# Which engine waits for the last store: the final wait of a row-sum kernel moved from SyncE to ScalarE

## Chip, cores, metric

One core of one Trainium2 chip. The metric is the device time of one execution in microseconds (us); all runs below are in the fast state, with a granted clock of 1.000. "Span" is the time from the first to the last instruction of the program in a profiled execution. The reported time is longer than the span, and that difference turns out to be what this case is about.

## The reference

```python
x = np.random.randn(32, 512, 1024).astype(np.float32)
relu_x = np.maximum(x, 0)
return np.sum(relu_x, axis=-1).astype(np.float32)
```

67.11 MB come in, 16,384 sums (0.07 MB) go out.

## The kernel before

SyncE issues all loads and all three stores. ScalarE clamps blocks in place and VectorE sums them; in the tail both take single rows with a fused sum. Loads raise one semaphore each, ScalarE raises `act`, VectorE raises `dve`, and the stores raise `stored`. At the end the kernel puts its semaphores back to zero. It writes that ending itself, without a barrier of its own:

```python
    # (cut: the body; n_stores is 3)
    nc.cur_bb = nc.bb_map[tc.start_bb_name + "_end"]
    nc.cur_bb.bb.instructions.clear()
    nums = sorted(s.num for s in (*sems.loads, sems.act, sems.dve))
    cleared = range(nums[0], nums[-1] + 1)
    assert len(cleared) == len(nums)
    nc.sync.sem_clear(cleared)
    nc.sync.wait_ge(sems.stored, 16 * n_stores).then_inc(sems.stored, -16 * n_stores)
    open_without_barrier(tc, EARLY)
    # (cut)

    # the end of the body (cut):
    act_row(buf[:, c + 3, :], m + 3, last_loaded)      # ScalarE's last work
    store(0, ROWS, *freed[0])
    store(ROWS, NT - ROWS - 2, *sums_done)
    # (cut: VectorE's last sums)
    store(NT - 2, 2, n_act, n_dve)                     # waits for act and dve
    return n_store
```

The clearing is safe where it stands: the last store of SyncE waits for all of `act` and `dve`, so nobody waits on a cleared semaphore any more.

## Time and profile before

| | before |
|---|---|
| reported time, three runs | 161.29 us (161.23 to 161.38) |
| reported time of the profiled run | 161.02 us |
| its span | 159.7 us (159.674 in the trace) |
| last sum of VectorE ends | 158.215 us |
| last store has landed | 159.641 us |
| SyncE's wait ends, the last instruction | 159.674 us |

The busy rows, the end of the chain and the two lines L45 and L46 are shown in the prediction below. How to read them: an instruction's duration does not contain the wait before it (L46 shows 17 ns, and SyncE's wait of 1.0 us stands as a gap in front of it). The profile's views show no instruction after the wait on L46.

### The profile page before, as it was taken

What the parts mean: (1) busy time and instruction counts of PE and PEld (TensorE: products, weight loads), DVE (VectorE), ACT (ScalarE), POOL (GpSimd) and SP (SyncE); (2) the same over time, 40 slices, a digit from 0 to 9 for tenths busy, and PEclk for the clock granted to TensorE, in tenths of its full rate; (3) what the DMA queues carried; (4) which work ended last, traced back from release to release, by engine and by line L of the source; (5) the groups of instructions that cost most, each with busy time, mean ns of one, the idle gap of its engine ahead of it and who ended that gap; (6) DMA issues with size and microseconds to landing.
All of it is one profiled execution on the core that took longest, in us unless ns stands there. A gap on an engine that the chain in (4) does not pass through costs nothing.

```text
span 159.7 us, 118 instructions
## 1 busy us (share of the span) xinstructions
DVE 117.5 (74%) x41; ACT 104.2 (65%) x50; POOL 0.2 (0%) x4
## 2 busy tenths in 40 slices
DVE  0000000009999499994999999999999999999986
ACT  3000059990799708996099941999339992499985
POOL 0000000000000000000000000000000000000000
DMA  8996996996996998979969969969969969898994
GB/s 279 509 525 263 525 525 263 525 525 263 525 493 296 525 410 378 525 345 443 525 263 525 525 263 525 525 263 525 525 263 525 525 263 525 345 443 386 409 408 126
DMA packets 2305, 67.18 MB, mean 421 GB/s; under 512 B 641, under 2 KB 897, under 8 KB 1025
## 3 DMA queue, kind: packets, MB, share of 16 engines
q1 hardware_dynamic: 2304, 67.18, 98.0%
q14 instruction: 1, 0.00, 0.0%
HBM read 67.11 MB, written 0.07 MB: 421 GB/s over the span
## 4 chain that ended last, share of the span: by engine, by line
DMA 43%; DVE 34%; ACT 17%; another core or an unknown queue 3%; SPq 1%; issue 0%; DVEq 0%
DMA io<-in_x_dram 43%; DVE res L123 32%; ACT io L115 17%; DVE io L140 1%; SPq L97 1%; DVE piece L219 0%; DVE piece L140 0%; DVEq L218 0%
## 5 line engine op out<-in xcount | busy, mean ns | idle before, releaser
L123 DVE TENSOR_REDUCE res<-io 128x8 f32<-128x8192 f32 (+2 forms) x9 | 101.1, 11287 | 39.9 <-ACT io L115 39.9
L115 ACT ACTIVATE io<-io 128x8192 f32<-128x8192 f32 (+2 forms) x9 | 81.7, 9110 | 47.6 <-DMA io<-in_x_dram 47.6
L130 ACT ACTIVATE io<-io 128x1024 f32<-128x1024 f32 x20 | 20.9, 1045 | 5.9 <-DMA io<-in_x_dram 5.7
L140 DVE TENSOR_SCALAR_CACHE_REDUCE io<-io 128x1024 f32<-128x1024 f32 (+1 forms) x14 | 15.5, 1165 | 0.7 <-DMA io<-in_x_dram 0.6
L130 ACT ACTIVATION_READ_ACCUMULATOR io<-io 128x1 f32 x20 | 3.8, 188 | 0.0
L115 ACT ACT_TABLE_LOAD x1 | 1.3, 1283 | 0.1
L140 DVE DVE_READ_ACCUMULATOR io<-io 128x1 f32 x14 | 1.1, 82 | 0.0
L219 DVE TENSOR_SCALAR_CACHE_REDUCE piece<-piece 128x406 f32<-128x406 f32 x1 | 0.6, 576 | 0.1
L140 DVE TENSOR_SCALAR_CACHE_REDUCE piece<-piece 128x260 f32<-128x260 f32 x1 | 0.4, 424 | 0.0
L264 POOL MEMSET const-bfloat16-1.0<- 128x1 bf16 x1 | 0.1, 101 | 0.0
L264 POOL MEMSET const-uint8-127<- 128x1 uint8 x1 | 0.1, 101 | 0.0
L264 POOL MEMSET const-float32-0.0<- 128x1 f32 x1 | 0.1, 98 | 0.2 <-issue 0.2
L264 POOL MEMSET const-float32-1.0<- 128x1 f32 x1 | 0.1, 98 | 0.0
L140 DVE DVE_READ_ACCUMULATOR piece<-piece 128x1 f32 x1 | 0.1, 83 | 0.0
L219 DVE DVE_READ_ACCUMULATOR piece<-piece 128x1 f32 x1 | 0.1, 83 | 0.0
## 6 DMA issues: line engine op xcount, KB each, us to landing
io<-in_x_dram SPq DMA_DIRECT2D x1, 4096.0 KB, 21.6
io<-in_x_dram SPq DMA_DIRECT2D x1, 2048.0 KB, 26.1
io<-in_x_dram SPq DMA_DIRECT2D x1, 1204.0 KB, 28.6
io<-in_x_dram SPq DMA_DIRECT2D x1, 512.0 KB, 29.4
piece<-in_x_dram SPq DMA_DIRECT2D x1, 202.0 KB, 29.3
piece<-in_x_dram SPq DMA_DIRECT2D x1, 130.0 KB, 29.3
io<-in_x_dram SPq DMA_DIRECT2D x7, 26.9
out_dram<-res SPq DMA_DIRECT2D x1, 55.0 KB, 1.6
```

The source lines that it names most:

```text
L97: dma = nc.sync.dma_start(out=dst, in_=src)
L115: i = nc.scalar.activation(out=ap, in_=ap, func=RELU)
L123: nc.vector.tensor_reduce(out=res[:, m : m + n], in_=ap, axis=mybir.AxisListType.X, op=ADD).wait_op(sems.act, n_act, "sem-ge").then_inc(se ...
L130: i = nc.scalar.activation(out=ap, in_=ap, func=RELU, accum_out=res[:, m : m + 1])
L140: i = nc.vector.tensor_scalar(out=ap, in0=ap, scalar1=0.0, scalar2=None, op0=MAX, op1=ADD, accum_out=accum_out,)
L219: nc.vector.tensor_scalar(out=last[:, :], in0=last[:, :], scalar1=0.0, scalar2=None, op0=MAX, op1=ADD, accum_out=res[:, NT - 2 : NT - 1],) ...
L264: nc = _bacc.Bacc("TRN2", target_bir_lowering=False, num_devices=1)
```

## The change

The wait for the stores, with its taking down of `stored`, goes from SyncE to ScalarE. SyncE's program then ends with the clearing. The evident intent is to let SyncE close its program while the store is still in flight.

```diff
     nc.sync.sem_clear(cleared)
-    nc.sync.wait_ge(sems.stored, 16 * n_stores).then_inc(sems.stored, -16 * n_stores)
+    nc.scalar.wait_ge(sems.stored, 16 * n_stores).then_inc(sems.stored, -16 * n_stores)
     open_without_barrier(tc, EARLY)
```

## The prediction

Its sum came to 161.29 - 0.07 = 161.22 us, its range to 160.9 to 161.5. The 0.07 us of the lean was worked out from no number.

> **What bounds the kernel now.** I first read the page, to see which resource is full over the whole span:
>
> ```profile
> span 159.7 us, 118 instructions
> DVE 117.5 (74%) x41; ACT 104.2 (65%) x50; POOL 0.2 (0%) x4
> ...
> DMA  8996996996996998979969969969969969898994
> ...
> q1 hardware_dynamic: 2304, 67.18, 98.0%
> ```
>
> Neither compute engine is full (74% and 65%), while the packets of the one queue take 98.0% of the time of 16 DMA engines. All the input, 67.11 MB of it, has to come in once, and the DMA row is high from the first slice to the last but one. The kernel is therefore bound by its loads, followed by a short tail: what has to be done with the last piece after it lands. A change can gain in the load stream or in that tail.
>
> The change touches only the last instructions, so I read the chain of work that ended last, at its end, and beside it the timeline of the last microseconds:
>
> ```profile
> 126.81 28.57 DMA io<-in_x_dram
> 155.39 0.02 issue
> 155.41 1.68 DVE io L140 x4
> 157.09 0.43 DVE piece L140 x2
> 157.51 0.03 issue
> 157.54 0.02 DVEq L218
> 157.56 0.07 issue
> 157.63 0.58 DVE piece L219 x2
> ```
>
> ```profile
> 157.67 0.18 ACT L130 ACTIVATION_READ_ACCUMULATOR io<-io 128x1 f32 x1
> 158.13 0.08 DVE L219 DVE_READ_ACCUMULATOR piece<-piece 128x1 f32 x1
> 158.24 0.33 SPq L108 DMA_DIRECT2D out_dram<-res  x1
> ```
>
> The chain's printed part stops with VectorE's last sum at 158.21, yet the span is 159.7: about 1.5 us follow. ScalarE is done at 157.67 + 0.18 = 157.85 and idle after that; VectorE's last read ends at 158.13 + 0.08 = 158.21; SyncE then issues the last store, from 158.24 to 158.57. What happens after this only the views of single lines show: the issues of DMAs with their time to landing, the two lines that the change touches (L45 is the clearing, L46 the wait), and SyncE's own waits:
>
> ```profile
> out_dram<-res SPq DMA_DIRECT2D x1, 1.0 KB, 1.4
> ```
>
> ```profile
> L45 SPq EVENT_SEMAPHORE_RANGE_CLEAR  x1: 58/58/58, 158.6 to 158.6; - x1
> ```
>
> ```profile
> L46 SPq EVENT_SEMAPHORE  x1: 17/17/17, 159.7 to 159.7; - x1
> ```
>
> ```profile
> SPq L46 <- SPq L46: 1.0, 1, 1.0
> ```
>
> The last store lands at about 158.24 + 1.4 = 159.64. SyncE clears the 15 load, act and dve semaphores at 158.6 in 58 ns, then waits 1.0 us for the landing, and its 17 ns instruction at 159.7 ends the program. The clearing lies wholly inside the flight of the store: it was already free.
>
> [...]L46 shows 17 ns, and the wait of 1.0 us only as a gap in front of it. [...]What there is, is a difference: the reported median is 161.29 us and the span 159.7, some 1.6 us more (1.3 us for the profiled execution itself, which took 161.02).
>
> **The change part by part.**
> Removed from SyncE: one wait with its update, L46. Its own duration is 17 ns, and the 1.0 us before it is waiting. It was the last instruction of SyncE, so nothing on SyncE comes earlier by its removal except the end of SyncE's program: from 159.67 to the end of the clearing, 158.6 + 0.06 = about 158.68, so 1.0 us earlier.
> Added to ScalarE: the same wait with the same update, behind its last read of the accumulator at 157.85. It gets to the wait about 159.64 - 157.85 = 1.8 us before the semaphore is full. Nothing of ScalarE's work lies behind it, and no work is delayed.
> Moved: the end of the program, from SyncE to ScalarE. How fast does ScalarE's sequencer wake? The trace before has no lone semaphore instruction on ScalarE, but it has three on SyncE (L107, 17 ns each) and one on VectorE (L218, 21 ns, 157.54, after the read that released it ended at about 157.50, so some 0.04 us of delay). For SyncE the same delay is 158.24 - 158.21 = 0.03 us at the last store; ScalarE's activations show a 0.02 us "issue" piece between a landing and a start in the chain. So the wake-up may differ by 0.00 to 0.02 us, and the instruction by 0.00 to 0.01 us.
> Not moved: all loads, all stores, every semaphore number, all work of VectorE and ScalarE before 157.85. The loads stay on SyncE's queue in the same order, and the store that is waited for is issued at the same moment by the same engine. The first 158.6 us should be the same in both traces.
> The sum inside the span: 159.67 + (-0.01 to +0.03) = 159.66 to 159.70, no change that 0.1% could show.
> Outside the span: the part after the last instruction can depend on which engine arrives last. [...]I lean to a small gain of some 0.07 us, for two reasons, neither of them in the trace: SyncE, which issued all the DMAs[...], is now free 1.0 us before the end, and someone who has already tuned the kernel moved the wait on purpose. 161.29 - 0.07 = 161.22.
>
> **The rivals.**
> (a) The clearing was on the path, and the change takes 1.0 us or more off the end. For it: by the trace SyncE's program does end 1.0 us earlier. Against it: the clear ends at 158.68 and the store lands at 159.64, and the program's end still needs that landing. If ending a program on SyncE cost much more than on ScalarE, all of the 1.3 us outside the span would be the most there is to win: 161.29 - 1.3 = 160.0, or -0.8%. Even this stays within 2%.
> (b) ScalarE is slow to end: [...]its own closing work is longer than SyncE's, and now it begins last. For it: before, ScalarE had 1.8 us between its last work and the end, in which any such thing was hidden. Against it: its sequencer merely waits, and by 159.64 its pipeline has been empty for 1.8 us.[...]
> (c) The load stream falls into another rhythm, because the program differs by one instruction per engine. For it: the load stream is 98% of the span, so a small share of it would outweigh all of the above. Against it: the difference comes after the last load, and the three runs before lie within 161.23 to 161.38. I give it the noise of runs, 0.1 to 0.2 us.
> (d) The early end of SyncE disturbs something that is still in flight, because its semaphores are cleared[...] before the store lands. The clearing was ahead of the landing before, too[...].
>
> **Range and chances.** The three runs before spread over 0.15 us. To this I add [...]a little more on the fast side for a part of rival (a) than on the slow side for (b): 160.9 to 161.5. To be faster by over 2% would need 3.2 us, twice all that lies behind VectorE's last sum within the span; to be slower by over 2% would need a new wait of 3.2 us, and nothing in the program makes one. I give each 0.6%, for surprises in the measurement.
>
> **What would show it right or wrong.** In the changed trace: the last loads land and VectorE's last read ends at 158.2 within 0.1 us; SyncE's last instruction is the clearing near 158.6, 58 ns long; a semaphore instruction of about 20 ns stands on ScalarE at 159.65 to 159.7 and is the last of all; the last store takes 1.4 us to land; the span is 159.7 within 0.1 us. If the span is equal and the reported time is not, the difference lies behind the program, in the order of arrival. The prediction is wrong if the time moves by more than 0.4 us: then ending on one engine costs more than on another, or the wait on ScalarE is satisfied later than the landing explains.

## The result

| | before | after |
|---|---|---|
| reported time, median of six fast runs each | 161.22 us (161.16 to 161.38) | 161.39 us (161.31 to 161.62) |
| span of the profiled run | 159.674 us | 159.866 us |
| its reported time minus its span | 1.35 us | 1.51 us |

Ratio 1.0011, interval 0.9998 to 1.0024: the same within 2%, and if anything slower. A ratio here is worked out from the single fast runs, so it is not quite the ratio of the medians.

First question: is it in the span? The page of the changed kernel has the same work and the same full DMA row:

```profile
span 159.9 us, 118 instructions
DVE 117.5 (74%) x41; ACT 104.2 (65%) x50; POOL 0.2 (0%) x4
...
DMA  8996996996997999989979969969969969898993
```

The chain of work that ended last (start, length, what), first of the kernel before and then of the changed one, says where most of the 0.19 us of span comes from:

```profile
0.43 40.65 DMA io<-in_x_dram
```

```profile
0.43 40.82 DMA io<-in_x_dram
41.25 0.02 issue
41.27 13.86 ACT io L115
...
126.99 28.58 DMA io<-in_x_dram
155.57 0.02 issue
155.59 1.68 DVE io L140 x4
157.27 0.43 DVE piece L140 x2
157.69 0.03 issue
157.72 0.02 DVEq L218
157.74 0.07 issue
157.81 0.58 DVE piece L219 x2
```

The wait for the first load is 0.17 us longer (40.82 against 40.65), and every later piece keeps its length: 28.58 against 28.57, 1.68 against 1.68, 0.43 against 0.43. The changed instruction stands 159 us after this. So most of the difference of these two spans comes in with the first load, and only a repetition can say whether that is chance.

Second, the end. These are the views of lines L45 and L46 and the last store's row among the DMA issues, of the changed kernel:

```profile
L45 SPq EVENT_SEMAPHORE_RANGE_CLEAR  x1: 58/58/58, 158.8 to 158.8; - x1
```

```profile
L46 ACTq EVENT_SEMAPHORE  x1: 17/17/17, 159.8 to 159.8; - x1
```

```profile
out_dram<-res SPq DMA_DIRECT2D x1, 1.0 KB, 1.4
```

As predicted: the clearing is SyncE's last instruction, the wait stands on ScalarE, takes 17 ns, and is the last of all; the store lands after the same 1.4 us. From the landing to the end of the wait the trace has 0.033 us before (159.641 to 159.674) and 0.038 us after (159.828 to 159.866). ScalarE wakes as fast as SyncE, to 5 ns.

Third, what lies behind the span. The packed trace lists only instructions that have a line of the program, and none stands there. But it keeps updates of semaphores, also of those that the program does not own (its own are 99 to 114). No view of `prof` prints them; they were read from the trace file itself. Semaphore 2 is such a one. These are its updates, in us from the end of the program's last instruction:

```
before, end 159.674:  three updates earlier, at 157.962, 158.001, 158.360 of the span, then
                      0.132 0.175 0.213 0.247 0.296 | 1.077 1.112 1.150 1.194 1.217 1.316 1.354 1.388 1.435
after,  end 159.866:  none earlier at the end of the program, then
                      0.139 0.178 0.222 0.245 0.343 0.383 0.417 0.463 | 1.248 1.283 1.321 1.364 1.388 1.487 1.525 1.559 1.606
```

Between the two groups most of the semaphores 7 to 255 get an update each (in the kernel before, from 0.26 to 0.85 us after the end). The trace does not say what semaphore 2 is for. The author took nine updates of it for one barrier, at which the engines wait for each other, and the passing from engine to engine for a walk; these are names for what the updates and e3 to e8 show, and nothing else about it is known here. The group on the right is a whole walk: nine updates in 0.358 us, on both kernels with the same steps to 1 ns. The one on the left is the same walk as far as it still had to go when the program ended. One more update of this walk stands at 0.449 us of the span, in both: an engine that has nothing to do had arrived at once. (TensorE has no instruction in either trace, and GpSimd's last ends at 0.43 us; that the update is TensorE's is shown by e5 below.)

So the author read the walk as one that visits the engines in a fixed order and waits at each for its end, which e3 to e5 then tested. Before, three engines had passed during the tail: updates at 157.962 (0.11 us after ScalarE's last work, 157.854), at 158.001 and at 158.360 (0.145 us after VectorE's, 158.215). That reads as TensorE (idle, at 0.449 us), ScalarE, GpSimd, VectorE, and then SyncE. When SyncE ended last, five updates were left, and the walk was done 0.296 us after the end. When ScalarE ended last, it was held at its second station, eight updates were left, and it was done after 0.463 us: 0.167 us more. After it, all takes the same 1.14 us in both (1.435 - 0.296 and 1.606 - 0.463). The two medians differ by as much (161.39 - 161.22 = 0.17), but that they agree so closely is partly luck: the same comparison gives 0.24 us in e2 and 0.05 us in e7 below. The part behind the span is steadier. The record gives every timed run's span, to 0.1 us; the mean of reported time minus span is 1.50 us over the six runs of the changed kernel, and 1.35 and 1.36 us over the two sets of nine runs of the kernel before on the chips of the experiments.

### The profile page after: what moved, and what is told of

Its sections match the earlier page's. It is cut to its first block, busy times and chain, and to the rows that moved or that the text cites. A ratio compares the mean times of both kernels' runs of the same rounds, so it can differ in the third digit from the quotient of the medians.

```text
span 159.9 us, 118 instructions
## 1 busy us (share of the span) xinstructions
DVE 117.5 (74%) x41; ACT 104.2 (65%) x50; POOL 0.2 (0%) x4
## 4 chain that ended last, share of the span: by engine, by line
DMA 43%; DVE 34%; ACT 17%; another core or an unknown queue 3%; SPq 1%; issue 0%; DVEq 0%
DMA io<-in_x_dram 43%; DVE res L123 32%; ACT io L115 17%; DVE io L140 1%; SPq L97 1%; DVE piece L219 0%; DVE piece L140 0%; DVEq L218 0%
```

## Experiments

**Theory A, the walk**: the order of the engines in the closing barrier makes the difference. Rivals: **B, the load stream**: the difference is chance in the first loads. **C, SyncE's early end**: it is not ScalarE's place that costs, but that SyncE closes while a store is in flight. And the prediction's own rival (b): ScalarE is slow to close. Each kernel below has the reference's output, and was right. In each, five runs were timed beside nine of the kernel before on the same chip. The first four kernels share one chip and its nine runs of before (median 161.14 us), the other four another (161.25 us). In the expectations "before" is the kernel before, and the times "to the release" and "to the end of the last barrier" count from the end of the program's last instruction to the last update of the left and of the right group above.

**e1: the kernel before against itself.** No edit.

> The kernel before, unchanged, against itself: the noise of the comparison. Theory A (the walk): the program is followed by a barrier that goes from engine to engine, seen in the trace as nine rises of one semaphore; with SyncE last, four of the nine lie before the last instruction's end or wait on nothing, so the time from the end of the program to the end of the last barrier is 1.43 us (1.435 in the trace of before) and reported time minus span 1.35 us. Theory B (the load stream): the 0.17 us between the two kernels is chance in the loads, so this run should itself scatter by 0.1 to 0.2 us in its span. Both: ratio 1.000 within 0.001.

Measured: 161.22 us, ratio 1.0004 (0.9992 to 1.0017). Its trace has the three early updates again, the release at 0.296 us and the end of the last barrier at 1.440. Its span is 160.031 us, 0.36 us longer than that of the same kernel above. Two pieces of its chain, the first load and a late one, say why:

```profile
0.42 40.91 DMA io<-in_x_dram
...
127.06 28.67 DMA io<-in_x_dram
```

The first is 0.26 us longer than above (40.65), the second 0.10 us (28.57).

So B is right about the span: the first load's 40.65 and 40.82 us of the two kernels, and 40.91 here, scatter by themselves: 0.26 us between two executions of one kernel, against 0.17 us between the two kernels. It is wrong about the part behind the span, which did not scatter: 1.435 and 1.440.

**e2: the changed kernel again.** No edit to it.

> The changed kernel, unchanged, on this chip and beside the others. Theory A: reported time minus span 1.51 us again, 0.17 us more than with SyncE last, and the median about 0.17 us above before (ratio 1.001). Theory B: minus the span the same as with SyncE last (1.35 us), and the median within 0.1 us of before.

Measured: 161.38 us, ratio 1.0013 (1.0000 to 1.0025), 0.24 us over the median of before. Release 0.463, end of the last barrier 1.608 us, reported time minus span 1.52. Here the span is 159.723, hardly longer than that of before in the first pair, and the loss is there all the same. A holds; B does not explain it.

**e3: the wait on VectorE.**

```diff
-    nc.scalar.wait_ge(sems.stored, 16 * n_stores).then_inc(sems.stored, -16 * n_stores)
+    nc.vector.wait_ge(sems.stored, 16 * n_stores).then_inc(sems.stored, -16 * n_stores)
```

> The wait stands on VectorE instead. Theory A with the order TensorE, ScalarE, GpSimd, VectorE, SyncE, read from the rises of the barrier's semaphore (ScalarE's own rise 0.139 us after the end, then 0.039, 0.044, 0.023 us, then 0.098 us for the turn and three more of about 0.04): VectorE last saves the steps of 0.039 and 0.044 us, so about 0.38 us from the end to the release instead of 0.46 (ScalarE) and 0.30 (SyncE); reported time minus span about 1.43 us. Rival C (whatever engine is late, any other engine than SyncE costs the same 0.17 us, because SyncE has ended early): 1.51 us. Theory B: 1.35 us.

Measured: 161.30 us, ratio 1.0013 (1.0000 to 1.0025). The view of L46 shows the wait where it should be:

```profile
L46 DVEq EVENT_SEMAPHORE  x1: 21/21/21, 159.7 to 159.7; - x1
```

Two updates (ScalarE, GpSimd) come early, at 157.989 and 158.028; six are left: 0.175 0.198 0.298 0.336 0.370 0.417. Against ScalarE's eight, the two steps of 0.039 and 0.044 us are gone, as expected, but VectorE's own first update comes after 0.175 us instead of 0.139. Hence 0.417 to the release instead of the expected 0.38, and 1.46 us of reported time minus span instead of 1.43. C wanted 1.51. Timed runs alone could not tell 1.46 from 1.51; the updates do.

**e4: the wait on GpSimd.** As e3, with `nc.gpsimd`.

> The wait stands on GpSimd. Theory A: one step of 0.039 us fewer than with ScalarE: about 0.42 us to the release, reported time minus span about 1.47 us, if GpSimd's sequencer wakes as fast as the others (its wake-up has no row yet; if slower, the span is longer too). Rival C: 1.51 us. Theory B: 1.35 us.

Measured: 161.64 us, ratio 1.0035 (1.0021 to 1.0049): the one kernel of this group with a clear loss, and a miss of all three expectations. The span is not the reason. The view of L46:

```profile
L46 POOLq EVENT_SEMAPHORE  x1: 17/17/17, 159.6 to 159.6; - x1
```

Of the early updates only TensorE's and ScalarE's (157.929) are left, so GpSimd stands behind ScalarE. GpSimd wakes as fast as the others (landing 159.619, end of the wait 159.661). But its own update of the barrier comes only 0.561 us after that, against 0.13 to 0.18 us on SyncE, ScalarE and VectorE. The rest of the walk then goes as A has it: 0.605 0.628 0.726 0.766 0.800 0.847, that is 0.286 us more in six steps (the same six in the changed kernel: 0.463 - 0.178 = 0.285). So A's steps are right, and a term was missing: each engine has a closing time of its own. C, the same cost for every engine, is dead. Where GpSimd spends 0.56 us, the trace does not show.

**e5: the wait on TensorE.** As e3, with `nc.tensor`.

> The wait stands on TensorE, which the barrier's order puts first. Theory A (the walk): all nine rises of the barrier's semaphore come after the program's end; from the first to the ninth they take 0.358 us (as in the barrier at the very end of every trace), and TensorE's own first rise takes 0.13 to 0.18 us as on SyncE, ScalarE and VectorE (0.56 us if it is as slow as GpSimd was): 0.49 to 0.54 us to the release, 1.63 to 1.68 us to the end of the last barrier, median 0.20 to 0.25 us above before. Rival C (every engine but SyncE costs the same 0.17 us because SyncE has ended early): 0.46 us and 1.61 us.

Measured: 161.61 us, ratio 1.0023 (1.0009 to 1.0036). The early update at 0.449 us of the span is gone, and all nine come after the end: 0.237 0.271 0.309 0.354 0.377 0.474 0.514 0.549 0.595. From first to ninth 0.358 us, as expected; TensorE's own 0.237 us was expected at 0.13 to 0.18, so the release (0.595) and the end of the last barrier (1.739) come later than the 0.49 to 0.54 and 1.63 to 1.68 expected. That the update at 0.449 us vanishes shows that it was TensorE's. The wait's own instruction is longer here, too:

```profile
L46 PEldq EVENT_SEMAPHORE  x1: 51/51/51, 159.9 to 159.9; - x1
```

From the landing to its end 0.080 us pass (159.911 to 159.991), against 0.033 in the kernel before. The median lies 0.36 us above before, more than the 0.20 to 0.25 expected: about 0.27 us of it lie behind the span (1.62 against 1.35), 0.05 in this slower waking, and the rest is within the scatter of the spans.

**e6: SyncE, first the wait, then the clearing.**

```diff
-    nc.sync.sem_clear(cleared)
     nc.sync.wait_ge(sems.stored, 16 * n_stores).then_inc(sems.stored, -16 * n_stores)
+    nc.sync.sem_clear(cleared)
```

> SyncE keeps both, in the other order: first the wait for the store, then the clearing. This puts the cost of the clearing on the path, which the prediction called free because it lay in the store's flight. Theory A: the clearing's 58 ns and a gap of about 0.04 us before it come on top: from the last landing to the end of the last barrier 1.57 us instead of 1.47, span and median 0.10 us longer than before, with the time from the program's end to the last barrier's end unchanged at 1.43 us. If the clearing cost nothing even there: no change. If ending right behind a clearing costs extra: more than 0.10 us.

Measured: 161.43 us, ratio 1.0010 (0.9997 to 1.0022). The view of each of the two lines:

```profile
L45 SPq EVENT_SEMAPHORE  x1: 17/17/17, 160.0 to 160.0; - x1
```

```profile
L46 SPq EVENT_SEMAPHORE_RANGE_CLEAR  x1: 52/52/52, 160.1 to 160.1; - x1
```

The wait ends at 160.003 and the clearing runs from 160.067 to 160.119, so 0.116 us come on top. From the landing (159.969) to the end of the last barrier (160.119 + 1.422 = 161.541) 1.572 us pass, against 1.468 before: 0.10 us more, as expected. The timed runs alone would not show it (the interval includes 1). So the clearing is worth 0.10 us when it lies behind the wait, and nothing where the kernel has it (158.620 to 158.678 us, in the flight of a store that lands at 159.641).

**e7: the changed kernel, with SyncE kept busy.**

```diff
-    nc.sync.sem_clear(cleared)
+    for _ in range(10):
+        nc.sync.sem_clear(cleared)
     nc.scalar.wait_ge(sems.stored, 16 * n_stores).then_inc(sems.stored, -16 * n_stores)
```

> The changed kernel, but SyncE clears the same semaphores ten times, which keeps it busy until shortly before the store lands, as it was in the kernel before; ScalarE still ends last. Theory A: the loss comes from where ScalarE stands in the walk, so it stays: 0.46 us to the release, 1.61 us to the end of the last barrier, median 0.17 us above before. Rival C (the early end of SyncE does the harm): 1.43 us and a median equal to before.

Measured: 161.30 us, ratio 1.0007 (0.9994 to 1.0019). The median is 0.05 us above before, nearer to what C expected (equal) than to A's 0.17; but the interval holds both, so it decides nothing by itself. The clearings fill the flight of the store:

```profile
L46 SPq EVENT_SEMAPHORE_RANGE_CLEAR  x10: 48/48/58, 158.8 to 159.5; - x10
```

SyncE ends at 159.576 instead of about 158.86; ScalarE's wait ends at 159.854. The release still comes 0.467 us after that and the end of the last barrier 1.612 us: the loss is whole. Reported time minus span says the same over all five timed runs: 1.50 us on average, against 1.36 of before on this chip. Keeping SyncE busy for 0.7 us more gave back nothing, so how early it ends is not what costs. (It still ended 0.24 us ahead of the landing, which came at 159.817, so this run does not try an end behind it. That C's loss would be one and the same for every engine is refuted by e3, e4 and e5.)

**e8: the kernel before, with ScalarE busy to shortly before the end.**

```diff
     act_row(buf[:, c + 3, :], m + 3, last_loaded)
+    for at, w in ((0, D), (D, D // 2)):
+        nc.scalar.activation(out=spare[:, at : at + w], in_=zeros[:, :w], func=RELU)
```

(`zeros` is set by GpSimd at the start behind one more semaphore, which ScalarE waits for before its first work and which SyncE clears with the others.)

> The kernel before, SyncE waits and ends last, but ScalarE gets two activations more into a spare buffer (1024 and 512 wide) and is busy until about 159.45 us, only 0.2 us before the program's end (before: 1.8 us). Theory A: ScalarE's rise at about 159.56, GpSimd's and VectorE's 0.04 and 0.08 us after it, all before SyncE's at 159.81: nothing is lost, 0.30 us to the release, 1.43 us to the end of the last barrier, median as before. Rival (b) of the prediction (ScalarE has some long closing work of its own, hidden before by its idle time): 0.1 to 0.3 us longer.

Measured: 161.25 us, ratio 1.0000 (0.9988 to 1.0013). The timeline of the end shows the added work, SyncE's last store beside it:

```profile
157.95 1.56 ACT L214 ACTIVATE spare<-zeros 128x1024 f32<-128x1024 f32 x2
158.33 0.08 DVE L226 DVE_READ_ACCUMULATOR piece<-piece 128x1 f32 x1
158.44 0.33 SPq L113 DMA_DIRECT2D out_dram<-res  x1
```

ScalarE ends at 159.512, the walk's next three updates come at 159.608, 159.646 and 159.690, and SyncE's wait ends at 159.871. Release 0.295, end of the last barrier 1.440: as before. ScalarE's own update comes 0.096 us after its work, so rival (b) has nothing. ScalarE was busy 1.56 us longer for nothing here, because its part of the walk was over before SyncE arrived.

All eight beside the two first kernels, by what the trace says behind the program's end (us):

| who ends last | own update | updates left | release | end of last barrier | reported minus span |
|---|---|---|---|---|---|
| SyncE (before; e1; e8) | 0.132; 0.132; 0.131 | 5 | 0.296; 0.296; 0.295 | 1.435; 1.440; 1.440 | 1.35 each |
| SyncE with a clearing (e6) | 0.119 | 5 | 0.284 | 1.422 | 1.33 |
| VectorE (e3) | 0.175 | 6 | 0.417 | 1.560 | 1.46 |
| GpSimd (e4) | 0.561 | 7 | 0.847 | 1.990 | 1.90 |
| ScalarE (after; e2; e7) | 0.139; 0.139; 0.145 | 8 | 0.463; 0.463; 0.467 | 1.606; 1.608; 1.612 | 1.51; 1.52; 1.52 |
| TensorE (e5) | 0.237 | 9 | 0.595 | 1.739 | 1.62 |

From the release to the end of the last barrier it is 1.14 us in all ten. The timed runs, spans to 0.1 us only, fit this: the mean of reported time minus span is 1.35 and 1.36 us (SyncE, kernel before), 1.31 (e6), 1.32 (e8), 1.49 (VectorE), 1.50, 1.53 and 1.50 (ScalarE), 1.64 (TensorE) and 1.90 (GpSimd); VectorE and ScalarE they do not tell apart. No ending tried beats the one that the kernel had.

## Why the prediction was right, and where its lean was wrong

Right: the range, "the same", and the place of the only term that counted. The steps on the span held: the loads and the tail do the same work, the last store takes the same 1.4 us, the clearing stays hidden (e6 measures what it would cost: 0.10 us), ScalarE's wake-up costs 5 ns more against the allowed 0 to 20. Its signs in absolute time did not hold: it wanted VectorE's end at 158.2 us, the wait at 159.65 to 159.7 and the span at 159.7, the first and last within 0.1 us, and the trace has 158.40, 159.85 and 159.87, because the first load took 0.17 us longer. It had allowed for the scatter of the loads in the reported time and not in these signs; e2, with 159.723, meets the one on the span. In the trace the store of 55 KB lands after 1.6 us, that of 1 KB after 1.4. Where in the flight these 1.4 us go, no run shows.

The step on the part outside the span named the right cause, that it depends on who comes last. The measured loss is 0.167 us, in these parts: three stations more had to be passed after ScalarE (0.039 + 0.044 + 0.023 = 0.106 us); the step behind SyncE took 0.098 us instead of 0.043 (0.055 us more), and the rest, about 6 ns, is ScalarE's own update and the last steps.

Wrong: the sign. The prediction leaned to a gain of 0.07 us where the loss is 0.167, on the thought that SyncE is now free 1.0 us before the end, and that a tuned kernel is not changed for nothing. The trace showed of neither that it gains anything. After a final wait SyncE closes as fast as any engine (0.13 us; the others 0.14 to 0.56), and e7 shows that its early end is worth nothing. What the prediction left out is where each engine stands in the walk: the order is fixed, and SyncE is the last of the five, so the kernel before already had the cheapest ending of those tried.

The working also stopped too early: it took the difference of reported time and span for all that there is on the part outside. The updates of semaphore 2 are in the trace. With the order read from the trace of before (one update at 0.449 us, two at 157.96 and 158.00 behind ScalarE's last work, one at 158.36 behind VectorE's, five behind SyncE's wait) the sign could have been told blind.

The rivals: (a) fell, since an earlier end of SyncE gains nothing (it ended at 158.86 us of a span of 159.87, and reported time minus span was 1.51 us against 1.35). (b) fell by e8 for ScalarE, though it is true of GpSimd (0.561 us). (c) is true of the scatter, and larger than thought: the spans of the ten profiled runs go from 159.66 to 160.12 us, of which e6's own 0.12 is one part and the first load the main other. Nothing in it belongs to the change. (d) did not show: all outputs were right.

Open: what each engine does between its final wait and its update of the barrier (0.13 to 0.56 us); why the walk's step behind SyncE is shorter when SyncE is last (0.043 against 0.098 us); and which engine makes each of the last four updates, for only the order of the first five was tested. (The expectation of e3 calls the step behind SyncE a turn; no trace shows that it is one.)

## What to carry to other kernels

The program's last instruction is not the end of the measured time: here 1.33 to 1.90 us of it lay behind that instruction, the engines closed one after the other in a fixed order, and the last wait was cheapest on SyncE, the last of them, and dearest on GpSimd (0.55 us more). All of this is at most 0.35% of this kernel's time. What went into the flight of the last store was free here, be it the clearing or 1.5 us of work on another engine that ended 0.36 us before the program did. For differences of 0.1% look at the part behind the span by itself: it repeats within 6 ns where the spans scatter by some 0.4 us.
